# One block on one core: weight buffers of 8 KB a partition, and the experts' weights in loads of 1 MB

## The chip, the cores and the metric

The kernel runs on 1 core of one Trainium2 chip. The metric is the device time of one execution in microseconds (us). The median of 3 runs is 1118.22 us (1117.07 to 1118.95).

## The reference

One decoder block on x of 512 tokens x 1024 channels, in float32. Three stages matter here.

- Projections: `u = RMSNorm(h)`, one wide product `u @ W_in`, a Mamba-2 SSD branch and a causal depthwise convolution branch on its columns, each with an output product, then the mixed result through `W_o`, added to h.
- Experts: `h + HierMoE(RMSNorm(h))`. A router picks one of 4 groups and two of its 8 experts for each token. An expert is `(silu(x @ w_gate) * (x @ w_up)) @ w_down` with inner width 512, so its three matrices are 2 MB each; 32 experts make 201.3 MB.
- Last stage: `h + (p @ W_ple_proj) * sigmoid(RMSNorm(h) @ W_ple_gate)`, then a final RMSNorm.

## The kernel before

The whole kernel is written out as a list of **units** (`unit`, L247). A unit has one or more weight loads and a function that issues its matmuls. `step` (L342) runs the units in order: it first splits the weights of later units, then lets `pump` (L261) issue loads, then the matmuls of its own unit, then `after` (L328) the jobs tied to that unit and as many of the floating `tasks` as a running credit allows. The order that comes out is the order on each engine; nothing reorders it later.

**Buffers.** All weights, and several other tiles, live in one pool of 22 **pages** of 4 KB a partition (`page`, L224; `PAGES`, L70). `state["room"]` counts the pages that `pump` may still fill with loads; `free(n)` gives n back or, with a negative n, takes them away. In the projections the room is 4 and later 8; before the experts it grows to 20.

**Two kinds of units.** In the projections and in the last stage a load of 512 KB (`raw`) is split in two parts: ACT casts it to the high part `wh` (`split_hi`, L275, the cast in L289), DVE subtracts to get the low part `wl` (`split_lo`, L293), each a page; PE then multiplies three times. The number of units that the split runs ahead is 2 in the projections and `BT["hi"]` = 6 from the experts on (L349). The experts' units are `plain`: PE reads the loaded float32 directly (L353 to L356) and the pages are freed after the unit's matmuls.

**Experts.** 32 experts stand in 7 groups of one or two quads; a quad is 4 strips of 32 slots, shared by 2 or 3 experts. For a quad there are 8 gate/up units (`gu_unit`, L1186: two matrices, four quarters of the contraction) and 4 down units (`d_unit`, L1199), each with one load of 512 KB per expert. With `(p k) n -> p k n` a load takes 4 KB that lie together for each partition. Between them stand, as jobs, `hid_act`, `hid_mul`, `hid_tr` (SiLU on ACT, product on DVE, transposition on PE) and `y_hi`, `y_lo` (scaled output on ACT and DVE); as tasks `disp` (tokens of the next group to slots), `back` and `combine` (the result back to tokens). `hot` writes the one-hot matrices of the next group, one page a group. The routing, `order0` to `order8`, are jobs of the first units (L1666). The first group's experts are fixed, the others are read from a register on SP.

**Before the last group** (one quad of three experts) come the two units of the ple projection (`p_unit`, L1308: 24 products each), and jobs that take room away: `free` of -1, -2, -8 and -4 pages (L1325 to L1341), since p, its parts and four output pages need pages.

**Last stage.** Eight units `e_unit` (L1431), 512 KB each: four for the first 512 columns, whose products run unit by unit, four for the second, whose products all run in the last unit (`prod`, token block by token block, k in order). The main body splits three of them between the transposes `e_tr` (L1812 to L1815). Behind the first half stand `e_gate` (tanh on ACT, two DVE instructions), `e_gain` on POOL and `e_sq` (a square on ACT).

All loads of weights go through SP's queue (L269), p and small tensors through POOL's. Matmuls, DVE copies and sums that go through a helper show as L120 in the profile.

Of the kernel before, what the change touches and what calls it, by code (L numbers as in the profile page):

```python
# [17 lines left out]
D = 1024  # L18
T = 512
# [47 lines left out]
    RANK[_b] = _i  # L67

_CST = {}
PAGES = 22  # L70
BT = dict(room=8, raw=20, hi=6, page=1.27, mm=1.75, cap=5.0, sp=5, fill=[1.8, 0.9], late=[14, 3])


TUNE = dict(
# [62 lines left out]
def tile_hybrid(ctx: ExitStack, tc: tile.TileContext, x, p, chan, rowv, rows, cst, w_in, w_ssd, w_conf, w_o,  # L137
# [83 lines left out]
            nc.scalar.copy(dsth, src)  # L221
            nc.vector.tensor_sub(dstl, src, dsth)

    def page(shape, dt):  # L224

        return st(shape, dt, "w", PAGES)

    def pages(n, dt):
        return Parts([page([128, 2, T], dt) for _ in range(n)], 2)

    al = slice(None)
    LAG = TUNE["lag"]
# [7 lines left out]
    jobs = defaultdict(list)  # L240
    state = {"pairs": 0, "n": 0, "load": 0, "room": 4, "split": 0, "lo": 0, "credit": 0, "top": 0}

    def load(src):
        loads.append(dict(src=src))
        return loads[-1]

    def unit(src, mms, cost=0.0, plain=False):  # L247
        srcs = [] if src is None else src if isinstance(src, list) else [src]
        units.append(dict(lds=[load(s) for s in srcs], mms=mms, cost=cost, plain=plain))
        return len(units) - 1  # L250

    def job(n, f, *a):
# [8 lines left out]
    def pump():  # L261
        while state["load"] < len(loads):
            ld = loads[state["load"]]
            if state["room"] <= 0:
                return
            src = ld["src"]()
            state["room"] -= 1
            ld["t"] = page([128] + list(src.shape[1:]), F32)
            nc.sync.dma_start(ld["t"], src)  # L269
            state["load"] += 1  # L270

# [3 lines left out]
    def split_hi():  # L275
        n = state["split"]
        if n >= len(units):
            return False
        u = units[n]
        if u["lds"] and not u["plain"]:  # L280
            ld = u["lds"][0]
            if "t" not in ld:
                pump()
            if "t" not in ld:
                assert n >= NB
                return False
            u["raw"] = ld["t"]
            u["wh"], u["wl"] = [page(list(u["raw"].shape), F32R) for _ in range(2)]
            nc.scalar.copy(u["wh"], u["raw"])  # L289
        state["split"] += 1  # L290
        return True
# [36 lines left out]
    def after(u):  # L328
        n = state["n"]
        issue(n - 0.5)  # L330
        issue(n)
        state["n"] = n + 1
        state["credit"] = min(state["credit"] + BT["page"] * len(u["lds"]) - u["cost"], BT["cap"])
        while True:
            t = min((t for t in tasks if t[0] <= n), key=lambda t: t[1], default=None)
            if t is None or (state["credit"] <= 0 and t[1] > n):
                break
            tasks.remove(t)
            state["credit"] -= t[2]
            t[3](*t[4])  # L340

    def step():  # L342
        n = state["n"]
        top = state["top"]
        if n < NB:
            while state["split"] <= min(max(n + 2, 2 * n - NB + BT["sp"]), top):
                split()
        else:
            while state["split"] <= min(top, n + BT["hi"]) and split_hi():  # L349
                split_lo()  # L350
        pump()
        u = units[n]
        if u["plain"]:  # L353
            ws = [ld["t"] for ld in u["lds"]]
            u["mms"](ws)
            free(len(ws))  # L356
        elif u["mms"] is not None:
            u["mms"](u["wh"], u["wl"])
        after(u)
# [44 lines left out]
        return first  # L404


    xl, xn = [Parts([page([128, D], F32) for _ in range(NT)], 1) for _ in range(2)]
    ss = st([128, NT], F32, "ss", 2)
    for c in range(NT):
        nc.sync.dma_start(xl[al, c, al], x[c * 128:(c + 1) * 128, :])  # L410
# [528 lines left out]
    def ln3(j):  # L939
        if j == 0:  # L940
            cm["h"] = pages(4, F32R)
            cm["l"] = []
        t = st([128, T], F32, "k2", 4)
        nc.vector.tensor_mul(t, cj[j], ln["rs"])
        nc.scalar.activation(t, t, AF.Silu, bias=ch("lnb", j), scale=ch("lng", j))
        nc.scalar.copy(cm["h"][al, j, al], t)
        if j < 6:
            cm["l"].append(st([128, T], F32R, "cj", 9))
        elif j == 6:
            lo = page([128, 2, T], F32R)  # L950
            cm["l"].extend(lo[:, i, :] for i in range(2))
        nc.vector.tensor_sub(cm["l"][j], t, cm["h"][al, j, al])

# [61 lines left out]
    pj = {}  # L1015

    def p_load():
        pj["p"] = page([128, NT, PLE], F32)
        nc.gpsimd.dma_start(pj["p"], p.rearrange("(c t) n -> t c n", t=128))

    def p_tr(k):
        pt = acc()
        for c in range(NT):
            nc.tensor.transpose(pt[:, c * 128:(c + 1) * 128], pj["p"][:, c, k * 128:(k + 1) * 128], ident)
        if k == 0:
            pj["h"], pj["l"] = [page([128, 2, T], F32R) for _ in range(2)]
        split_t(pj["h"][:, k, :], pj["l"][:, k, :], pt, None)

    def p_mm(c, wh, wl):
# [6 lines left out]

    def p_out(n, c):
        if c % 2 == 0:
            pj["o", n, c // 2] = page([128, 2, T], F32)
        nc.scalar.activation(pj["o", n, c // 2][:, c % 2, :], pj.pop("s"), AF.Copy, scale=0.5)  # L1040

    NO = len(units)
# [143 lines left out]
    def gu_unit(gi, q, i, kp):  # L1186
        quad = GROUPS[gi][q]

        def mms(ws):
            if kp == 0:  # L1190
                PG[gi, q, i] = acc()
            x = XT[gi, kp]
            for kk in range(2):
                strips(PG[gi, q, i], x[:, kk, q * QS:(q + 1) * QS], [w[:, kk, :] for w in ws], quad,
                       kp == 0 and kk == 0, kp == 3 and kk == 1)
        return unit([lambda b=m[0]: weights((eg, eu)[i], b)[:, 2 * kp:2 * kp + 2, :] for m in quad], mms, BT["mm"],
                    True)

    def d_unit(gi, q, f):  # L1199
        quad = GROUPS[gi][q]  # L1200

        def mms(ws):
            if f == 0:
                PY[gi, q] = [acc2(), acc2()]
            for n in range(2):
                strips(PY[gi, q][n], HT[gi, q][:, f, :], [w[:, 0, n * 512:(n + 1) * 512] for w in ws], quad, f == 0,
                       f == 3)
        return unit([lambda b=m[0]: weights(ed, b)[:, f:f + 1, :] for m in quad], mms, BT["mm"], True)

    def hid_act(gi, q):  # L1210
        t = st([128, DE], F32, "k2", 4)
# [9 lines left out]
    def hid_tr(gi, q):  # L1221
# [4 lines left out]
        nc.scalar.copy(t, pt.rearrange("p (f s) -> p f s", s=QS))  # L1226
        HT[gi, q] = t

    def hot(gi, q):
        if q == 0:  # L1230
            G["oh", gi] = page([128, NT, 2 * QS], F32R)
        for b, j0, ns in GROUPS[gi][q]:
            r = ns * ST
            o = q * QS + j0 * ST
            nc.vector.tensor_tensor(G["oh", gi][:, :, o:o + r], cs_("slot")[:, None, :r].to_broadcast([128, NT, r]),
                                    R["pos"][:, :, b:b + 1].to_broadcast([128, NT, r]), op=OP.is_equal)

    def hot_first(c):

        if c == 0:  # L1240
            G["oh", 0] = page([128, NT, 2 * QS], F32R)
        w = [128, 4, 2 * ST]
        nc.vector.tensor_tensor(G["oh", 0][:, c].rearrange("p (j s) -> p j s", s=2 * ST),
                                cs_("slot")[:, None, :2 * ST].to_broadcast(w),
# [70 lines left out]
    def fill_now(room):  # L1315
        fill_pe(state["n"], room)

    combined = NB + 9
    for gi, g in enumerate(GROUPS):
        last = gi == len(GROUPS) - 1  # L1320
        first = len(units)
        if last:
            for n in range(2):
                p_unit(n)
            job(first - 10, free, -1)  # L1325
            job(first - 9, p_load)
            job(first - 8, free, -2)
            for k in range(2):
                job(first - 4 + k, p_tr, k)
            job(first - 3, free, -8)  # L1330
        for q in range(len(g)):
            for kp in range(4):
                for i in range(2):
                    u = gu_unit(gi, q, i, kp)
            job(u - 1, hid_act, gi, q)
# [2 lines left out]
            job(u, hid_tr, gi, q)  # L1338
            job(u, fill_now, BT["fill"][1])
            if last:  # L1340
                job(u - 3, free, -4)  # L1341
            for f in range(4):
                u = d_unit(gi, q, f)
            task(combined, u - 1, 1.4, back, gi, q)
            for n in range(2):
                job(u, y_hi, gi, q, n)
                job(u, y_lo, gi, q, n)
# [4 lines left out]
            continue  # L1352
        for n in range(2):
            for c in range(NT):
                task(u + 1, u + 9, 0.23 * 2 * len(g), combine, gi, c, n)
        combined = u + 10
        o = first + (BT["late"][0] if gi == 0 else BT["late"][1])
        for q in range(len(GROUPS[gi + 1])):
            job(o + q, hot, gi + 1, q)
        for kp in range(4):  # L1360
            task(o + 2, u, 0.115 * 16, disp, gi + 1, kp)
    for i in range(3):
        unit(None, None)
    NC = len(units)
# [45 lines left out]

    def e_gain(c):

        E["o", c] = page([128, D], F32)
        ns = slice(0, 512)
        nc.gpsimd.tensor_mul(E["o", c][:, ns], hh_["h"][:, c, ns], E["gf"][:, ns])

# [247 lines left out]

    state["top"] = NE
    for i, f in enumerate((order0, order4, order1, order2, order3, order5, order6, order7, order8)):  # L1666
        job(NB + 2 + i, f)
    pts = [acc() for _ in range(4)]
    for a in range(2):
        for k in range(4):  # L1670
            disp_mm(0, k, pts[k], a)
    for k in range(4):
        disp_out(0, k, pts[k])
        step()
        step()
    run(NC)

    W32 = [128, NEXP]
# [207 lines left out]
```

## Time and profile before

| | us |
|---|---|
| median of 3 runs | 1118.22 |
| lowest, highest | 1117.07, 1118.95 |
| the profiled execution, its own time | 1116.51 |
| its span (first to last instruction) | 1114.8 |
| PE, DVE, ACT busy in the span | 1029.8, 561.6, 345.1 |
| HBM read | 252.83 MB |

The mean granted TensorE clock is 0.982 of full speed. An engine's busy time is a mean over stages with different limits, so it is read stage by stage: projections to about 526 us, routing to 542 us, experts to about 1055 us, last stage to the end. Ends of matmuls are modelled, so a busy PE is not a PE at its peak.

### The profile page before, as it was taken

The page shows a single profiled execution, that of the slowest core. Times are in us where ns is not written, and L with a number is a line of the kernel's source. Part 1 is how long each engine was busy: PE and PEld are TensorE (multiplying, and loading weights), DVE is VectorE, ACT ScalarE, POOL GpSimd, SP SyncE. Part 2 cuts the span into 40 slices and gives each one's busy share as a digit, 9 for nine tenths or more (in the row PEclk, how much of TensorE's full clock was granted, in tenths as well). Part 3 has the DMA queues.
Part 4 walks back from the last instruction along what each step waited for, and adds up shares of the span by engine and source line. Part 5 has one row for each costly group of instructions (what it writes and reads, how often), then busy time and mean ns, then how long its engine had stood idle before and what let it go on. Part 6 is the DMA issues. An engine that isn't in the chain of part 4 may idle for free. (4 is left out here: it accounts for less than half of the span.)

```text
span 1114.8 us, 16449 instructions
## 1 busy us (share of the span) xinstructions
PE 1029.8 (92%) x6262; PEld 665.0 (60%) x6262; DVE 561.6 (50%) x1004; ACT 345.1 (31%) x646; POOL 14.7 (1%) x32
## 2 busy tenths in 40 slices
PE   5999999999989999997999999989989899659796
PEld 4788899877868887886553434425335235125375
DVE  6689998897889955655322203112021121021475
ACT  5443356767442245334111100101101101021263
POOL 1000000000000000000000000000000000000011
PEclk9999999999999999999899999999999999969998
DMA  9323232202223341373599899999999999968801
GB/s 268 101 82 87 79 94 59 76 19 76 76 57 107 95 148 66 127 302 113 192 409 359 304 411 408 409 409 409 408 409 408 409 409 409 404 241 328 319 24 75
DMA packets 123314, 256.04 MB, mean 230 GB/s; under 512 B 7856, under 2 KB 65216, under 8 KB 123232
## 3 DMA queue, kind: packets, MB, share of 16 engines
q1 hardware_dynamic: 122544, 252.74, 61.6%
q0 software_dynamic: 688, 2.22, 0.7%
q8 instruction: 50, 0.82, 0.3%
q14 instruction: 32, 0.26, 0.1%
HBM read 252.83 MB, written 2.10 MB: 229 GB/s over the span
## 5 line engine op out<-in xcount | busy, mean ns | idle before, releaser
L120 PE MATMUL acc<-uh,w 128*128 128x512 f32 x704 | 230.5, 400 | 0.8 <-DVE ul L120 0.8
L120 PE MATMUL acc<-w,cj 128*32 128x512 f32 x1664 | 214.7, 596 | 8.1 <-DMA w<-eu 4.3
L120 PE MATMUL acc<-w,uh 128*128 128x256 f32 (+2 forms) x752 | 162.1, 325 | 1.1 <-DVE w L120 0.9
L120 PEld LDWEIGHTS acc<-uh,w 128*128 128x128 f32 x704 | 132.3, 188 | 31.2 <-issue 1.7
L120 PE MATMUL acc<-w,m 128*32 128x512 f32 (+1 forms) x960 | 133.2, 569 | 10.2 <-ACT m L1226 5.3
L120 DVE TENSOR_TENSOR w<-w 128x1024 fp32r<-128x1024 f32 x86 | 104.4, 1220 | 75.6 <-ACT w L289 62.9
L120 PE MATMUL acc<-ul,w 128*128 128x512 f32 x352 | 137.4, 390 | 0.0
L120 PEld LDWEIGHTS acc<-w,cj 128*32 128x32 f32 x1664 | 52.2, 109 | 140.2 <-issue 94.1
L120 PEld LDWEIGHTS acc<-w,uh 128*128 128x128 f32 x752 | 118.2, 193 | 26.3 <-issue 15.3
L120 DVE SCALAR_TENSOR_TENSOR cj<-glu,chan,cj 128x512 f32<-128x512 f32 x180 | 130.8, 747 | 2.2
L120 PE MATMUL acc<-w,ul 128*128 128x256 f32 (+2 forms) x488 | 117.3, 307 | 0.6 <-DVE ul L120 0.6
L289 ACT CAST w<-w 128x1024 fp32r<-128x1024 f32 x86 | 89.6, 1054 | 75.1 <-PE acc L120 44.1
L120 PE MATMUL acc<-w 128*128 128x512 f32 x384 | 98.9, 394 | 3.1 <-ACT w L289 2.4
L120 PEld LDWEIGHTS acc<-w,m 128*32 128x32 f32 (+1 forms) x960 | 43.4, 122 | 82.8 <-issue 44.3
L120 DVE TENSOR_TENSOR k<-k,acc 128x512 f32<-128x512 f32 x21 | 19.1, 910 | 138.9 <-PE acc L120 138.8
L120 PEld LDWEIGHTS acc<-w 128*128 128x128 f32 x384 | 71.5, 188 | 21.4 <-ACT w L289 2.8
L120 DVE TENSOR_TENSOR Z<-Z,acc 128x512 f32<-128x512 f32 x64 | 43.3, 686 | 79.9 <-PE acc L120 79.9
L120 PEld LDWEIGHTS acc<-w,ul 128*128 128x128 f32 x488 | 77.0, 188 | 6.8 <-DVE ul L120 1.4
L120 PEld LDWEIGHTS acc<-ul,w 128*128 128x128 f32 x352 | 66.2, 188 | 14.9 <-issue 1.7
L1258 ACT COPY cj<-acc 128x512 f32<-128x512 f32 (+1 forms) x28 | 15.6, 556 | 163.4 <-PE acc L120 163.4
L120 PE MATMUL acc<-ident,k 128*128 128x128 f32 x116 | 17.9, 282 | 28.6 <-DVE k L120 26.8
L120 DVE SCALAR_TENSOR_TENSOR w<-glu,chan,w 128x512 f32<-128x512 f32 x60 | 42.9, 747 | 0.7
(267 smaller groups left out, 864.6 us busy)
## 6 DMA issues: line engine op xcount, KB each, us to landing
w<-eg SPq DMA_DIRECT2D x128, 512.0 KB, 10.1
w<-eu SPq DMA_DIRECT2D x128, 512.0 KB, 10.1
w<-ed SPq DMA_DIRECT2D x128, 512.0 KB, 10.1
w<-w_in SPq DMA_DIRECT2D x52, 512.0 KB, 3.7
w<-w_ssd_out SPq DMA_DIRECT2D x8, 512.0 KB, 3.9
w<-w_conf_out SPq DMA_DIRECT2D x8, 512.0 KB, 3.6
w<-w_o SPq DMA_DIRECT2D x8, 512.0 KB, 3.5
w<-w_ple_gate SPq DMA_DIRECT2D x8, 512.0 KB, 10.3
```

The costliest lines, as they stand in the source:

```text
L120: return f(*a, **k)
L289: nc.scalar.copy(u["wh"], u["raw"])
L1258: nc.scalar.copy(t, pt[:, :2 * w].rearrange("p (k s) -> p k s", k=2))
```

## The change

The pool becomes 11 buffers of 8 KB a partition. `page` hands out halves: the first request with a key takes a buffer, the second with the same key takes its other half. `wh` and `wl` of one unit share a buffer, so do two consecutive raw loads, pairs of `x`, of the outputs `po` and `eo`, and so on. The experts' loads are `wide`: 1 MB each, a whole buffer, 8 KB together for each partition, two pages of room. There are half as many experts' units, each twice as large (4 gate/up and 2 down units a quad). The one-hot matrices of all groups live in the two halves of one buffer. The numbers that count in units are set anew: `hi` 6 to 1, `late`, the due units of the tasks, the jobs of the routing, and the frees before the last group.

```diff
-PAGES = 22
-BT = dict(room=8, raw=20, hi=6, page=1.27, mm=1.75, cap=5.0, sp=5, fill=[1.8, 0.9], late=[14, 3])
+PAGES = 11
+BT = dict(room=8, raw=20, hi=1, page=1.27, mm=3.5, cap=5.0, sp=5, fill=[1.8, 0.9], late=[7, 2])
...
-    def page(shape, dt):
-
-        return st(shape, dt, "w", PAGES)
+    pend = {}
+
+    def page(shape, dt, key):
+        v = pend.pop(key, None)
+        if v is None:
+            v = st([128, 4 * T], dt, "w", PAGES)
+            pend[key] = v[:, 2 * T:]
+            v = v[:, :2 * T]
+        return v.rearrange("p (a b) -> p a b", b=shape[2]) if len(shape) == 3 else v
...
-            if state["room"] <= 0:
+            if state["room"] <= (1 if ld["wide"] else 0):
                 return
             src = ld["src"]()
-            state["room"] -= 1
-            ld["t"] = page([128] + list(src.shape[1:]), F32)
+            if ld["wide"]:
+                state["room"] -= 2
+                ld["t"] = st([128] + list(src.shape[1:]), F32, "w", PAGES)
+            else:
+                state["room"] -= 1
+                ld["t"] = page([128] + list(src.shape[1:]), F32, "raw")
             nc.sync.dma_start(ld["t"], src)
...
-            u["wh"], u["wl"] = [page(list(u["raw"].shape), F32R) for _ in range(2)]
+            u["wh"], u["wl"] = [page(list(u["raw"].shape), F32R, n) for _ in range(2)]
...
-            free(len(ws))
+            free(2 * len(ws))
...
-        return unit([lambda b=m[0]: weights((eg, eu)[i], b)[:, 2 * kp:2 * kp + 2, :] for m in quad], mms, BT["mm"],
+            for kk in range(4):
+                k = 4 * kp + kk
+                strips(PG[gi, q, i], XT[gi, k // 2][:, k % 2, q * QS:(q + 1) * QS], [w[:, kk, :] for w in ws], quad,
+                       k == 0, k == KD - 1)
+        return unit([lambda b=m[0]: weights((eg, eu)[i], b)[:, 4 * kp:4 * kp + 4, :] for m in quad], mms, BT["mm"],
...
-        return unit([lambda b=m[0]: weights(ed, b)[:, f:f + 1, :] for m in quad], mms, BT["mm"], True)
+        return unit([lambda b=m[0]: weights(ed, b)[:, 2 * fp:2 * fp + 2, :] for m in quad], mms, BT["mm"], True)
...
+    def one_hot(gi):
+        if gi == 0:
+            G["ohs"] = st([128, 2, NT, 2 * QS], F32R, "w", PAGES)
+        return G["ohs"][:, gi % 2]
...
-            job(first - 10, free, -1)
-            job(first - 9, p_load)
-            job(first - 8, free, -2)
+            job(first - 6, free, -2)
+            job(first - 5, p_load)
+            job(first - 5, free, -2)
             for k in range(2):
-                job(first - 4 + k, p_tr, k)
-            job(first - 3, free, -8)
+                job(first - 3 + k, p_tr, k)
+            job(first - 2, free, 2)
+            job(first - 2, free, -8)
...
             if last:
-                job(u - 3, free, -4)
-            for f in range(4):
+                job(u - 1, free, -2)
+            for f in range(2):
                 u = d_unit(gi, q, f)
             task(combined, u - 1, 1.4, back, gi, q)
+            if last:
+                job(u - 1, free, -2)
...
-            job(o + q, hot, gi + 1, q)
+            job(o, hot, gi + 1, q)
...
-        job(NB + 2 + i, f)
+        job(NB + (i + 1) // 2, f)
```

## Rows read from the trace of the kernel before

**Rows 1.** The page, part 2: DMA busy tenths and GB/s in 40 slices.
```profile
DMA  9323232202223341373599899999999999968801
GB/s 268 101 82 87 79 94 59 76 19 76 76 57 107 95 148 66 127 302 113 192 409 359 304 411 408 409 409 409 408 409 408 409 409 409 404 241 328 319 24 75
```

**Rows 2.** Stretches: length, busy us (count) of PE, PEld, DVE, ACT, POOL; PEclk, DMA share, GB/s.
```profile
20.00:526.00 506.00, 496.78 (x2528) 409.12 (x2526) 405.58 (x645) 234.30 (x457) 2.97 (x9) 1.00 0.33 102
...
542.00:597.00 55.00, 51.60 (x444) 23.13 (x440) 10.59 (x40) 7.76 (x14) 0.00 (x0) 0.97 0.98 382
597.00:645.00 48.00, 48.00 (x385) 22.95 (x378) 12.25 (x26) 6.77 (x11) 0.00 (x0) 1.00 0.91 330
645.00:965.00 320.00, 300.15 (x2147) 122.22 (x2146) 52.35 (x106) 34.59 (x58) 0.76 (x1) 1.00 1.03 408
965.00:987.00 22.00, 2.52 (x12) 0.38 (x10) 3.38 (x3) 2.09 (x2) 0.00 (x0) 0.66 0.86 330
987.00:1020.00 33.00, 32.02 (x200) 16.49 (x200) 5.04 (x8) 7.92 (x13) 0.00 (x0) 0.91 0.72 249
1020.00:1045.00 25.00, 23.54 (x166) 9.60 (x162) 5.11 (x10) 1.77 (x3) 0.00 (x0) 1.00 1.03 409
```

**Rows 3.** Waits, 645 to 966 us: engine, line, waited for, us in total, times, longest.
```profile
PEld acc L120 <- DMA w<-ed: 23.4, 28, 1.1
```

**Rows 4.** The chain that ended last, one piece: start, us, what.
```profile
1059.58 34.47 PE acc L120 x155
```

**Rows 5.** Waits, 966 to 990 us.
```profile
DVE w L120 <- ACT w L289: 34.7, 1, 34.7
...
PE acc L120 <- DVE k L120: 19.5, 1, 19.5
ACT w L289 <- DMA w<-w_ple_proj: 18.5, 1, 18.5
```

**Rows 6.** DMA packets: 13:29 (512 B), 1044:1050 (2 KB), 700:900 us (4 KB).
```profile
DMA packets 9210, 4.64 MB, mean 290 GB/s; under 512 B 144, under 2 KB 9210, under 8 KB 9210
...
DMA packets 1203, 2.32 MB, mean 387 GB/s; under 512 B 72, under 2 KB 72, under 8 KB 1203
...
DMA packets 22408, 81.75 MB, mean 409 GB/s; under 512 B 2489, under 2 KB 2489, under 8 KB 22392
```

**Rows 7.** The page, part 6, DMA issues: KB each, us from issue to landing.
```profile
w<-eg SPq DMA_DIRECT2D x128, 512.0 KB, 10.1
...
w<-w_o SPq DMA_DIRECT2D x8, 512.0 KB, 3.5
...
w<-p POOLq DMA_DIRECT2D x1, 512.0 KB, 8.1
```

**Rows 8.** Timeline, PE, 762 us: start, us, instruction.
```profile
762.06 5.36 PE L120 MATMUL acc<-w,cj 128*32 128x512 f32 x48
```

**Rows 9.** Timeline, ACT and DVE, last stage: start, us, instruction, idle before.
```profile
1058.09 1.04 ACT L289 CAST w<-w 128x1024 fp32r<-128x1024 f32 x1
...
1081.53 0.69 ACT L1406 ACTIVATE k<-acc,et 128x512 f32<-128x512 f32 x1 [0.17 <-PE acc L120]
1082.93 0.69 ACT L1406 ACTIVATE k<-acc,et 128x512 f32<-128x512 f32 x1 [0.71 <-PE acc L120]
...
1089.23 0.63 ACT L1372 ACTIVATE k<-Z 128x512 bf16<-128x512 f32 x1 [1.54 <-DVE Z L120]
...
1057.64 1.23 DVE L120 TENSOR_TENSOR w<-w 128x1024 fp32r<-128x1024 f32 x1
...
1081.54 0.69 DVE L120 TENSOR_TENSOR Z<-Z,k 128x512 f32<-128x512 f32 x1
...
1087.51 1.69 DVE L120 TENSOR_TENSOR Z<-Z,k 128x512 f32<-128x512 f32 x1
```

**Rows 10.** One more stretch, columns as in rows 2.
```profile
530.00:540.00 10.00, 10.00 (x64) 9.75 (x64) 7.52 (x21) 1.76 (x3) 0.00 (x0) 0.74 0.01 2
```

**Rows 11.** Waits of PE, 20 to 526 us.
```profile
PE acc L120 <- ACT w L289: 2.4, 1, 2.4
```

More of the change, by code (lines that the diff above doesn't have):

```diff
@@ L222, in split_t @@
             nc.vector.tensor_sub(dstl, src, dsth)
-    def page(shape, dt):
-        return st(shape, dt, "w", PAGES)
+    pend = {}
[6 more added lines that the diff above has]
+        return v.rearrange("p (a b) -> p a b", b=shape[2]) if len(shape) == 3 else v
     def pages(n, dt):
-        return Parts([page([128, 2, T], dt) for _ in range(n)], 2)
+        k = object()
+        return Parts([page([128, 2, T], dt, k) for _ in range(n)], 2)
     al = slice(None)
@@ L241, in tile_hybrid, with load @@
     state = {"pairs": 0, "n": 0, "load": 0, "room": 4, "split": 0, "lo": 0, "credit": 0, "top": 0}
-    def load(src):
-        loads.append(dict(src=src))
+    def load(src, wide):
+        loads.append(dict(src=src, wide=wide))
         return loads[-1]
@@ L248, in unit @@
         srcs = [] if src is None else src if isinstance(src, list) else [src]
-        units.append(dict(lds=[load(s) for s in srcs], mms=mms, cost=cost, plain=plain))
+        units.append(dict(lds=[load(s, plain) for s in srcs], mms=mms, cost=cost, plain=plain))
         return len(units) - 1
@@ L332, in after @@
         state["n"] = n + 1
-        state["credit"] = min(state["credit"] + BT["page"] * len(u["lds"]) - u["cost"], BT["cap"])
+        state["credit"] = min(state["credit"] + BT["page"] * (2 if u["plain"] else 1) * len(u["lds"]) - u["cost"], BT["cap"])
         while True:
@@ L404, in tokproj @@
         return first
-    xl, xn = [Parts([page([128, D], F32) for _ in range(NT)], 1) for _ in range(2)]
+    xl, xn = [Parts([page([128, D], F32, "x") for _ in range(NT)], 1) for _ in range(2)]
     ss = st([128, NT], F32, "ss", 2)
@@ L949, in ln3 @@
         elif j == 6:
-            lo = page([128, 2, T], F32R)
+            lo = page([128, 2, T], F32R, "lo")
             cm["l"].extend(lo[:, i, :] for i in range(2))
@@ L1017, in p_load @@
     def p_load():
-        pj["p"] = page([128, NT, PLE], F32)
+        pj["p"] = page([128, NT, PLE], F32, "p")
         nc.gpsimd.dma_start(pj["p"], p.rearrange("(c t) n -> t c n", t=128))
@@ L1025, in p_tr @@
         if k == 0:
-            pj["h"], pj["l"] = [page([128, 2, T], F32R) for _ in range(2)]
+            pj["h"], pj["l"] = [page([128, 2, T], F32R, "ph") for _ in range(2)]
         split_t(pj["h"][:, k, :], pj["l"][:, k, :], pt, None)
@@ L1038, in p_out @@
         if c % 2 == 0:
-            pj["o", n, c // 2] = page([128, 2, T], F32)
+            pj["o", n, c // 2] = page([128, 2, T], F32, "po")
         nc.scalar.activation(pj["o", n, c // 2][:, c % 2, :], pj.pop("s"), AF.Copy, scale=0.5)
@@ L1191, in mms, with d_unit @@
                 PG[gi, q, i] = acc()
[L1192 to L1195, printed above, removed]
-        return unit([lambda b=m[0]: weights((eg, eu)[i], b)[:, 2 * kp:2 * kp + 2, :] for m in quad], mms, BT["mm"],
+            for kk in range(4):
[3 more added lines that the diff above has]
+        return unit([lambda b=m[0]: weights((eg, eu)[i], b)[:, 4 * kp:4 * kp + 4, :] for m in quad], mms, BT["mm"],
                     True)
-    def d_unit(gi, q, f):
+    def d_unit(gi, q, fp):
         quad = GROUPS[gi][q]
         def mms(ws):
-            if f == 0:
+            if fp == 0:
                 PY[gi, q] = [acc2(), acc2()]
-            for n in range(2):
-                strips(PY[gi, q][n], HT[gi, q][:, f, :], [w[:, 0, n * 512:(n + 1) * 512] for w in ws], quad, f == 0,
-                       f == 3)
-        return unit([lambda b=m[0]: weights(ed, b)[:, f:f + 1, :] for m in quad], mms, BT["mm"], True)
+            for f in (2 * fp, 2 * fp + 1):
+                for n in range(2):
+                    strips(PY[gi, q][n], HT[gi, q][:, f, :], [w[:, f % 2, n * 512:(n + 1) * 512] for w in ws], quad,
+                           f == 0, f == 3)
+        return unit([lambda b=m[0]: weights(ed, b)[:, 2 * fp:2 * fp + 2, :] for m in quad], mms, BT["mm"], True)
     def hid_act(gi, q):
@@ L1227, in hid_tr @@
         HT[gi, q] = t
+    def one_hot(gi):
+        if gi == 0:
+            G["ohs"] = st([128, 2, NT, 2 * QS], F32R, "w", PAGES)
+        return G["ohs"][:, gi % 2]
     def hot(gi, q):
         if q == 0:
-            G["oh", gi] = page([128, NT, 2 * QS], F32R)
+            G["oh", gi] = one_hot(gi)
         for b, j0, ns in GROUPS[gi][q]:
@@ L1240, in hot_first @@
         if c == 0:
-            G["oh", 0] = page([128, NT, 2 * QS], F32R)
+            G["oh", 0] = one_hot(0)
         w = [128, 4, 2 * ST]
@@ L1316, in fill_now @@
         fill_pe(state["n"], room)
-    combined = NB + 9
+    combined = NB + 4
     for gi, g in enumerate(GROUPS):
@@ L1324, in tile_hybrid @@
                 p_unit(n)
-            job(first - 10, free, -1)
-            job(first - 9, p_load)
-            job(first - 8, free, -2)
+            job(first - 6, free, -2)
+            job(first - 5, p_load)
+            job(first - 5, free, -2)
             for k in range(2):
-                job(first - 4 + k, p_tr, k)
-            job(first - 3, free, -8)
+                job(first - 3 + k, p_tr, k)
+            job(first - 2, free, 2)
+            job(first - 2, free, -8)
         for q in range(len(g)):
-            for kp in range(4):
+            for kp in range(2):
                 for i in range(2):
@@ L1354, in tile_hybrid @@
             for c in range(NT):
-                task(u + 1, u + 9, 0.23 * 2 * len(g), combine, gi, c, n)
-        combined = u + 10
+                task(u + 1, u + 5, 0.23 * 2 * len(g), combine, gi, c, n)
+        combined = u + 5
         o = first + (BT["late"][0] if gi == 0 else BT["late"][1])
         for q in range(len(GROUPS[gi + 1])):
-            job(o + q, hot, gi + 1, q)
+            job(o, hot, gi + 1, q)
         for kp in range(4):
-            task(o + 2, u, 0.115 * 16, disp, gi + 1, kp)
+            task(o + 1, u, 0.115 * 16, disp, gi + 1, kp)
     for i in range(3):
@@ L1411, in e_gain @@
     def e_gain(c):
-        E["o", c] = page([128, D], F32)
+        E["o", c] = page([128, D], F32, "eo")
         ns = slice(0, 512)
@@ L1673, in tile_hybrid @@
         disp_out(0, k, pts[k])
-        step()
-        step()
+        if k % 2:
+            step()
+            step()
     run(NC)
```

## The prediction

> **What bounds the kernel now.** I read the slices of the page first: three stages show. Up to some 525 us the DMA is mostly idle, from there to 1045 us most slices move 400 GB/s and more, and in the last 60 us the DMA rests again [rows 1]. The table by stretches says which engine sets the pace in each [rows 2]. From 20 to 526 us PE is busy 496.78 of 506 us: the projections are bound by TensorE, and the loads hide behind it. From 542 to 645 us the stream of the experts' weights runs at 382 and 330 GB/s while PE hardly pauses: PE holds the 20 pages, and the loads wait for room. From 645 to 965 us the stream runs at 408 GB/s without a gap, and TensorE waits for loads, 23.4 us for ed's alone [rows 3]: here the DMA is the bound. From 965 to 1020 us it falls to 330 and 249 GB/s, then it is back at 409 to 1045 us. The last 60 us are a chain through PE, ACT and DVE, with 34.47 us of uninterrupted matmuls in it [rows 4].
>
> The hole at 965 us is an order on two engines: six units ahead of the ple projection the split of its weights is queued. ACT waits 18.5 us for that load, DVE 34.7 us behind ACT, and the multiply of the hidden layer stands behind DVE's subtract, so PE waits 19.5 us [rows 5]. When it resumes, buffers come free too slowly to fill the queue.
>
> **The change part by part.** The sum is made against the profiled execution (1116.51 us, span 1114.8), which lies 1.7 us under the median of 1118.22; a difference is carried over to the median.
>
> *Rows of 8 KB.* 384 loads of 512 KB become 192 of 1 MB, with 8 KB instead of 4 KB together in each partition. No row shows 8 KB, so I extend the three sizes that ran back to back on all 16 engines: 512 B at 290 GB/s, 2 KB at 387, 4 KB at 409 [rows 6]. Time of one row on one engine, 16 x size / rate: 28.2, 84.7 and 160.2 ns. From 512 B to 2 KB each KB adds 37.6 ns, from 2 to 4 KB 37.8 ns: a straight line with some 9 ns fixed. Four more KB give 160.2 + 151.0 = 311.2 ns, so 421 GB/s. What can gain is the stream behind the stretch that PE holds: 202.4 MB (experts and the projection's 1.05) less the 20 pages of 0.524 MB held at 542 us, 55 us x 382 and 48 us x 330, which leaves 155.1 MB. At 409 GB/s that is 379.2 us, at 421 it is 368.4: **-10.8 us**. Bounds: 0 (a row moves as two of 4 KB) and -13.4 (424 GB/s, if more than the row's fixed part goes with the smaller number of loads). I take 421, since both steps of size lie on one line.
>
> The Trainium skill (DMA: Bandwidth & Descriptors, Bandwidth, "Why small descriptors are slow") puts the fixed cost at about 3 cycles a packet beside one cycle for 32 bytes; a 4 KB row then loses 2.3%, and 8 KB would win 1.2%, as an estimate 4.3 us in place of 10.8, and the time would be 1117.1. The trace disagrees so far: 3 cycles beside 128 are 3.5 ns of a row's 151, and its fixed part is 9.
>
> *Issue.* SP starts half as many loads. Their issue hides behind a queue that is 10.1 us from issue to landing against 3.5 us for an unqueued load [rows 7]; without that cover it would be a fraction of a microsecond a load. A wide load waits until two pages of room are there, and what stands behind it on SP waits with it; that is counted in the tail below. I take 0.
>
> *Split one unit ahead (hi 6 to 1), the frees before the last group.* ACT's cast for the projection now comes just before the last down unit, after the hidden layer's work of that quad, so the 19.5 us wait of PE goes. Behind the waiting cast stand now y_hi on ACT and y_lo on DVE, for which only the later combines wait. What is late next is room. A wide unit costs PE 3.6 us (48 matmuls take 5.36 us, 16 of them one old unit, [rows 8]). By hand, at 421 GB/s, time 0 being the landing of the first down unit's third load in the last but one group: the loads pumped so far keep the stream going to 12.5 us; PE ends the two down units at 3.2 and 10.7 us; room is now 10 pages, five buffers, while a unit of this quad takes three. The projection's two units are 24 products each, 5.6 us (six take 1.40 us, [rows 9]), and hold PE to 22 us, when the five buffers are full. The first gate unit ends at 25.7 us, and a load starts 2.1 us after its issue (3.5 less 1.36 us of transfer): a gap of 5.4 us. Each later release leaves a smaller one: 1.3 before the last up load, 2.8 and 2.8 us at the down loads, as room shrinks to four and three buffers. Together 12.3 us of idle DMA. Before it was 22 us x (1 - 330/409) + 33 us x (1 - 249/409) = 17.2 us [rows 2]. The last unit is 3.6 us instead of 1.8, which adds 1.6 us behind its last landing. **-3.3 us**, between -10 (gaps hidden by the tasks between the units) and +3.
>
> *Split one unit ahead, last stage.* The same number rules the splits here. Before, all eight weights of the gate product were split in its first steps; now only the first four are (main asks for them between the e_tr), and those of the second half come one a step. The third and fourth of the second half then stand on DVE behind the two instructions of each of the four e_gate, on ACT behind their four tanh and, the fourth, behind the four squares of e_sq; PE's first product waits for them, and everything to the end waits for PE. PE ends the first half at 1082.9 us (the last tanh starts on it). It needs the third low part 13 products later, at 1085.9 us. DVE ends the e_gate at 1087.51 + 1.69 = 1089.20 us and its subtract takes 1.23: 1090.4 us, a wait of 4.5 us. Beside POOL's multiply the adds took 1.69 us instead of 0.69, so the subtract may take 1 us more. The fourth: ACT's last square starts at 1089.23 us, then a cast of 1.04 and the subtract, some 0.5 us behind PE again [rows 9]. I take **+5.5 us** (4.5 to 6.5). Behind such a pause the granted clock may be at the lower level: in the 10 us after the routing's pause it averaged 0.74, 2.6 us lost at most [rows 10]; I take **+1.0 us**.
>
> *8 KB buffers in the projections.* Halves of one buffer come free together: a raw half up to one unit (5.6 us) later, with four loads ahead and 3.5 us to landing. The high and low weights of one unit end with the same matmuls. I take 0; PE's pauses cover it, and without them each late cast would be PE's wait. The nearest row is one wait of 2.4 us for a cast in 506 us [rows 11], so 0 to +4.
>
> *The rest.* The routing jobs, one-hots and dispatches keep their place within about 1 MB of weights, in a stretch that PE holds (542 to 645 us): 0, between -3 and +3. The load of p on POOL has two wide units, some 15 us, to land; it took 8.1 [rows 7]. The one-hots' shared buffer and both halves at one job: 0, DVE is mostly idle there.
>
> Sum: -10.8 - 3.3 + 5.5 + 1.0 = -7.6; 1116.5 becomes 1108.9, and on the median 1110.6 us.
>
> **The rivals.** *8 KB rows are no faster.* The fixed part of a row may belong to something that does not halve. For it: nothing here has moved 8 KB rows in a stream, and 2 to 4 KB gave only 6%; against it: the line. Then -3.3 + 6.5 = +3.2: **1121.4**, slower. It decides below 412.6 GB/s, where the rate wins under 3.2 us. The skill's 3 cycles would leave it just above that point.
>
> *The late splits are hidden.* If PE is paced by something else in the second half 6.5 us fall away: **1104.1**. For it: DVE has little queued behind the e_gate; against it: PE's 34.47 us without a break.
>
> *The shared buffers hold the projections back.* 76 casts; each late by 0.10 us eats the gain, at 0.2 us the time is **1126**. Against it: PE's pauses total 9 of 506 us.
>
> *The clock falls in the stream.* With three loads a unit PE's bursts come 2.5 us apart instead of 1.3. At the lower level (1.2 of 2.4 GHz) a group's 24 quarter units (43 us) and the rest would take some 120 us where the stream needs 75, over four groups some +180: **1285**. Against it: the clock stayed at 1.00 through 320 us of short bursts [rows 2]. The Trainium skill (TensorE: Matmul & The Clock Gate, Part 1) has the clock halve when the array idles; here it was 0.66 around a 20 us pause and 1.00 between bursts.
>
> **How the numbers follow.** Forecast 0.52, no faster rows 0.20, hidden splits 0.18, held projections 0.07, clock 0.03. The likeliest case alone runs from 1102 to 1117 (bounds of its tail and waits). The range must reach both neighbours: 1099 to 1122. A measurement of this kernel tells about 0.2% (2.2 us) from nothing. Faster 0.66: 0.46 of the forecast, the hidden splits, 0.02 of the others. Same 0.09: 0.05 of the forecast, the rest from rows only a little faster. Slower 0.25: the other two rivals and most of the case without faster rows.
>
> **What would show it.** Between 650 and 950 us the GB/s read 421; the same 409 kills the first term. Packets in a stretch of the stream halve, and none lies under 8 KB but the small ones. ACT's wait for the ple projection is a few us, PE's wait on the multiply of the hidden layer is about 1 us. Holes of 1 to 6 us in the DMA up to the last down load. In the last stage a wait of PE for DVE's w of some 5 us, 25 us before the end; its absence puts the second rival right. From 20 to 526 us PE busy within 3 us of before. I am wrong if the stream is at 421 and the time is not under 1116, or if it is at 409 and the time is.

## The result and the profile after

The changed kernel takes 1109.47 us (median of 4 runs, 1109.12 to 1111.59) beside 1117.64 us of the kernel before in the same session: a ratio of **0.9926** (95% interval 0.9911 to 0.9941), 8.2 us less. The prediction was 1110.6 us. The profiled execution took 1109.12 us with a span of 1107.4. The total came out as forecast; its parts did not.

The page of the changed kernel, part 2: DMA busy tenths and GB/s in 40 slices.

```profile
DMA  9323232202224323265199999999999999999401
GB/s 268 99 69 107 77 87 67 77 1 77 68 65 118 86 77 114 77 234 222 39 382 388 392 376 423 420 421 421 421 421 420 421 421 420 418 377 422 178 1 76
```

Beside [rows 1] the plateau is higher, 420 to 423 in place of 408 to 411, and the dent at its end is nearly gone (418, 377, 422 where before had 404, 241, 328, 319). The stretches of [rows 2], in the changed kernel (columns as there):

```profile
20.00:526.00 506.00, 495.41 (x2487) 407.03 (x2486) 400.00 (x619) 229.70 (x447) 2.97 (x9) 0.99 0.33 99
542.00:597.00 55.00, 53.04 (x448) 27.77 (x450) 14.53 (x55) 10.19 (x16) 0.00 (x0) 0.95 0.76 308
597.00:645.00 48.00, 47.22 (x384) 22.24 (x380) 11.22 (x21) 5.78 (x10) 0.00 (x0) 1.00 0.95 376
645.00:965.00 320.00, 288.66 (x2222) 129.00 (x2215) 54.16 (x112) 36.17 (x62) 0.76 (x1) 0.98 1.01 419
965.00:987.00 22.00, 18.97 (x112) 8.57 (x105) 6.28 (x7) 6.88 (x11) 0.00 (x0) 1.00 1.02 416
987.00:1020.00 33.00, 31.13 (x210) 16.77 (x212) 7.15 (x13) 4.62 (x8) 0.00 (x0) 0.98 0.95 389
```

The first row is a trap, and the prediction fell into it: PE is as busy as before, yet it has done less, 2487 matmuls in place of 2528 (and DVE 619 instructions in place of 645). A window of fixed times can't show that work has moved out of it. So I cut every profile at two instructions instead: ACT's one instruction on `prev` in the routing, and the 16 transposes that open the last stage. The changed kernel's timeline has them at

```profile
537.41 0.20 ACT L1558 ACTIVATE prev<-prev 128x16 f32<-128x16 f32 x1
...
1038.65 3.00 PE L120 MATMUL acc<-ident,Z 128*128 128x128 f32 x16 [3.53 <-DVEq L1704]
```

and the timeline of the kernel before at

```profile
527.80 0.20 ACT L1536 ACTIVATE prev<-prev 128x16 f32<-128x16 f32 x1
...
1055.29 1.97 PE L120 MATMUL acc<-ident,Z 128*128 128x128 f32 x16 [2.22 <-DVEq L1681]
```

Cut so, for every kernel of this study (us, one profiled execution each; ratio of the timed runs to before's beside them, with its 95% interval):

| kernel | up to routing | routing to last stage | last stage | span | ratio |
|---|---|---|---|---|---|
| before | 527.8 | 527.5 | 59.5 | 1114.8 | 1 |
| changed | 537.4 | 501.2 | 68.8 | 1107.4 | 0.9926 (0.9911 to 0.9941) |
| last_splits | 538.1 | 505.4 | 59.8 | 1103.2 | 0.9867 (0.9850 to 0.9883) |
| room3 | 530.7 | 502.6 | 68.6 | 1101.8 | 0.9862 (0.9838 to 0.9885) |
| rows4 | 538.5 | 514.4 | 68.8 | 1121.7 | 1.0037 (1.0017 to 1.0057) |
| two_loads | 536.3 | 511.8 | 68.6 | 1116.6 | 1.0001 (0.9991 to 1.0010) |
| both_fix | 529.0 | 505.2 | 59.7 | 1093.8 | 0.9777 (0.9753 to 0.9801) |
| split_early | 537.5 | 504.6 | 68.6 | 1110.7 | 0.9938 (0.9915 to 0.9962) |
| before_hi1 | 530.8 | 511.0 | 60.0 | 1101.7 | 0.9862 (0.9837 to 0.9887) |
| before_room3 | 530.3 | 527.1 | 59.6 | 1117.0 | 0.9995 (0.9983 to 1.0008) |

The change wins 26.3 us in the experts' stage, where 14.1 were forecast, and loses 9.6 in the projections (0 forecast) and 9.2 in the last stage (6.5). Below, a difference of two ratios is turned into us by the 1118 us of before; with these intervals it is good to 2 to 4 us. A stage's length comes from one execution: last_splits has the changed kernel's program up to the last stage, and its experts' stage was 4.1 us longer, so lengths in this table are good to some 4 us.

### The profile page after: what moved, and what is told of

Its sections match the earlier page's. It is cut to its first block, busy times and chain, and to the rows that moved or that the text cites. A ratio compares the mean times of both kernels' runs of the same rounds, so it can differ in the third digit from the quotient of the medians.

```text
span 1107.4 us, 15682 instructions
## 1 busy us (share of the span) xinstructions
PE 1017.9 (92%) x6262; PEld 675.5 (61%) x6262; DVE 562.2 (51%) x1004; ACT 344.6 (31%) x646; POOL 15.5 (1%) x32
## 5 line engine op out<-in xcount | busy, mean ns | idle before, releaser
L120 PE MATMUL acc<-w,cj 128*32 128x512 f32 x1664 | 203.4, 608 | 17.6 <-DMA w<-eu 10.7
L120 PEld LDWEIGHTS acc<-w,cj 128*32 128x32 f32 x1664 | 56.2, 112 | 143.3 <-issue 105.3
L120 PE MATMUL acc<-w,m 128*32 128x512 f32 (+1 forms) x960 | 126.8, 574 | 13.7 <-DMA w<-ed 8.8
L120 PE MATMUL acc<-w 128*128 128x512 f32 x384 | 102.0, 405 | 3.0 <-ACT w L302 2.4
L120 PEld LDWEIGHTS acc<-w 128*128 128x128 f32 x384 | 74.0, 194 | 22.0 <-ACT w L302 2.8
L1226 ACT ACTIVATE k<-acc 128x512 f32<-128x512 f32 x13 | 7.8, 598 | 165.2 <-PE acc L120 165.2
L1277 ACT COPY cj<-acc 128x512 f32<-128x512 f32 (+1 forms) x28 | 15.6, 555 | 81.9 <-PE acc L120 81.9
```

The lines of the kernel that those rows point to most:

```text
L120: return f(*a, **k)
L1226: nc.scalar.activation(t, PG.pop((gi, q, 0)), AF.Silu)
L1277: nc.scalar.copy(t, pt[:, :2 * w].rearrange("p (k s) -> p k s", k=2))
```

## The experiments

### The row or the load: rows4 and two_loads

Loads of 1 MB whose partition rows are two runs of 4 KB:

```diff
-        return unit([lambda b=m[0]: weights((eg, eu)[i], b)[:, 4 * kp:4 * kp + 4, :] for m in quad], mms, BT["mm"],
+        def src(b):
+            w = weights((eg, eu)[i], b)
+            return w.rearrange("p (a c b) n -> p c a (b n)", a=2, c=2)[:, kp] if gi else w[:, 4 * kp:4 * kp + 4, :]
+        return unit([lambda b=m[0]: src(b) for m in quad], mms, BT["mm"],
...
-        return unit([lambda b=m[0]: weights(ed, b)[:, 2 * fp:2 * fp + 2, :] for m in quad], mms, BT["mm"], True)
+        return unit([lambda b=m[0]: weights(ed, b)[:, fp::2, :] for m in quad], mms, BT["mm"], True)
```

The order of the products follows the rows (those lines are left out here).

> The changed kernel, its loads still 1 MB each and as many, but of two runs of 4 KB a partition instead of one of 8 KB (the first group's gate and up weights stay as they are). Theory of the row: the rate follows the row, so the stream between 700 and 950 us falls from 421 to 409 GB/s and the time rises by 8 to 11 us, to 1117.5 to 1120.5. Rival (the load): the rate follows the size of the load, so it stays near 421 and the time within 2 us of 1109.5.

And the same buffers filled by two loads each:

```diff
-            nc.sync.dma_start(ld["t"], src)
+            if ld["wide"]:
+                m = src.shape[1] // 2
+                for i in range(2):
+                    nc.sync.dma_start(ld["t"][:, i * m:(i + 1) * m], src[:, i * m:(i + 1) * m])
+            else:
+                nc.sync.dma_start(ld["t"], src)
```

> The changed kernel, each buffer of 1 MB filled by two loads of 512 KB with rows of 4 KB, issued one behind the other. Both theories of the rate give 409 GB/s between 700 and 950 us and 1117.5 to 1120.5 us; against the kernel with two runs of 4 KB in one load it tells what the number of loads costs by itself: 0 if the issue is hidden, up to 3 us where the queue starts from empty behind the routing and in the last group.

The DMA between 700 and 940 us, in the changed kernel (packets; then issues: KB each, us to landing):

```profile
DMA packets 13849, 100.96 MB, mean 421 GB/s; under 512 B 1539, under 2 KB 1539, under 8 KB 1539
...
w<-eg SPq DMA_DIRECT2D x32, 1024.0 KB, 15.2
```

in rows4

```profile
DMA packets 25395, 98.08 MB, mean 409 GB/s; under 512 B 1493, under 2 KB 1493, under 8 KB 25378
...
w<-eg SPq DMA_DIRECT2D x31, 1024.0 KB, 15.8
```

and in two_loads

```profile
DMA packets 26892, 98.10 MB, mean 409 GB/s; under 512 B 2987, under 2 KB 2987, under 8 KB 26874
...
w<-eg SPq DMA_DIRECT2D x63, 512.0 KB, 10.2
```

The rate follows the row, and the load's size does nothing to it: 409 GB/s with loads of 1 MB and of 512 KB alike, 421 with 8 KB together. rows4 is 12.4 us slower than the changed kernel, two_loads 8.4 us; 8 to 11 were expected of both. That the two differ by 4 us I had not expected; it is the other way round from a cost of issue, and stays open.

### The last stage: last_splits

```diff
-            while state["split"] <= min(top, n + BT["hi"]) and split_hi():
+            while state["split"] <= min(top, n + (6 if n >= NE else BT["hi"])) and split_hi():
```

> The changed kernel with one edit: in the last stage alone the split runs 6 units ahead again, as before. Theory: the four splits that stand behind the squares and the gate's DVE pairs cost PE one wait of 6.5 us for DVE's w at 1070 us, and the clock after it 1 to 2 us more; so the wait goes and the time falls by 6.5 to 8.5 us, to 1101 to 1103 us. Rival: the first half's squares and the adds on DVE (1.68 us beside POOL) pace the stage whatever the order; then PE waits for something else instead and the time falls by less than 3 us.

What it was to remove, in the changed kernel. Waits of PE, 1036 to 1108 us:

```profile
PE acc L120 <- DVE w L120: 6.5, 1, 6.5
```

The timeline of its DVE behind the first half's products:

```profile
1061.92 1.23 DVE L120 TENSOR_TENSOR w<-w 128x1024 fp32r<-128x1024 f32 x1 [5.00 <-ACT w L302]
...
1073.52 1.67 DVE L120 TENSOR_TENSOR Z<-Z,k 128x512 f32<-128x512 f32 x1
1075.11 1.21 DVE L120 TENSOR_TENSOR w<-w 128x1024 fp32r<-128x1024 f32 x1
```

and of its PE:

```profile
1069.33 0.50 PE L120 MATMUL acc<-w,uh 128*128 128x512 f32 x1
1076.37 0.80 PE L120 MATMUL acc<-w,uh 128*128 128x512 f32 x1 [6.55 <-DVE w L120]
```

The third subtract of the second half starts as the last add of the gate ends, and PE starts as the subtract ends: the step the prediction named. ACT's timeline of last_splits has the four casts ahead of the squares:

```profile
1049.48 2.95 ACT L302 CAST w<-w 128x1024 fp32r<-128x1024 f32 x3
...
1054.28 1.05 ACT L302 CAST w<-w 128x1024 fp32r<-128x1024 f32 x1
```

Of the waits of PE, 1043 to 1104 us, only the one for the stage's first input is left:

```profile
PE acc L120 <- DVEq L1704: 3.5, 1, 3.5
```

The stage is back at 59.8 us, 9.0 less; the ratio gives 6.6 us, at the lower end of the 6.5 to 8.5 expected. The span falls by only 4.2 us, since the experts' stage of this execution was 4.1 us longer.

### The projections: room3 and before_room3

Where the 9.6 us are lost is read from the casts `w <- w` on ACT. In the changed kernel's timeline they come in pairs, one late, one at once:

```profile
339.47 1.05 ACT L302 CAST w<-w 128x1024 fp32r<-128x1024 f32 x1 [6.30 <-PE acc L120]
...
342.39 1.05 ACT L302 CAST w<-w 128x1024 fp32r<-128x1024 f32 x1 [1.37 <-DVE w L120]
...
409.77 1.04 ACT L302 CAST w<-w 128x1024 fp32r<-128x1024 f32 x1 [5.34 <-PE acc L120]
412.77 0.63 ACT L928 ACTIVATE k<-cj 128x512 f32<-128x512 f32 x1 [1.95 <-DVE cj L120]
```

and PE's, behind the last of these:

```profile
413.45 1.05 PE L120 MATMUL acc<-ones,k 128*128 128x1 f32 x8 [2.93 <-ACT k L928]
```

The cast itself is rarely what PE wants. What PE wants stands behind it, on two engines: DVE waits 7.16 us for the cast at 409.77 before it can subtract, the input of the square of L928 stands on DVE behind that subtract, so the square starts 1.95 us after the cast has ended, and PE waits 2.9 us for the square. Behind the wait PE's matmuls are slower for a while, 12 of them in 4.59 us (granted clock 0.68 from 413.4 to 418.8 us) where 7 of the same shape, six microseconds later, take 1.85:

```profile
414.37 4.59 PE L120 MATMUL acc<-w 128*128 128x512 f32 x12
...
420.50 1.85 PE L120 MATMUL acc<-w 128*128 128x512 f32 x7
```

Matched with the kernel before matmul by matmul, the lag of PE is 1.0 us up to 309 us, 3.4 from 310, 4.9 from 340 and 9.6 from 418: it comes in steps, not with each cast. The first and the third step (1.0 and 1.5 us) are no doing of the change, as the last section shows. The second (2.4 us, with a wait of PE of 1.6 us for DVE's `w`) and the fourth (4.7 us, the wait of 2.9 and the slow matmuls behind it) stand in all five kernels that have the changed projections as they are (2.3 to 2.4 and 4.7 to 5.5 us) and in no other: some 7 us. Waits of PE, 270 to 435 us, in the changed kernel:

```profile
PE acc L120 <- ACT k L928: 2.9, 1, 2.9
...
PE acc L120 <- DVE w L120: 2.1, 2, 1.6
```

My theory counts buffers. From unit 33 on `ssd_norm` holds eight pages, `late` and `gate_sig1` two each; loads may have 4, and three units' high and low weights 6: 22 pages exactly, 11 buffers exactly. But a raw pair keeps its buffer until its second half is split, so four pages of loads can sit in three buffers. Then one unit's weights are a buffer short, and its cast waits for PE. One page less for loads should cure it:

```diff
-            job(n, free, 2)
+            job(n, free, 3)
...
     job(0, halve)
+    job(30, free, -1)
```

> The changed kernel with one edit: from unit 30 of the projections to the end of the SSD output product, loads may hold 3 pages instead of 4. Theory: pairs of raw loads that share a buffer hold up to three buffers where room counts two, so every second cast on ACT waits some 7 us for PE to end a unit, and what stands behind the cast makes PE wait; with one page less the casts' waits for PE fall from 54.6 us to under 20, the projections end 4 to 7 us earlier, and the time is 1103 to 1106 us. Rival: loads come too late with three pages; then the casts wait for the DMA instead and the time is 1109 to 1113. Second rival: the 9.6 us are mostly the clock's; then no change within 1.5 us.

Waits of ACT, 270 to 425 us, in the changed kernel:

```profile
ACT w L302 <- PE acc L120: 52.0, 9, 7.5
```

and in room3:

```profile
ACT w L302 <- DVE w L120: 35.0, 5, 7.8
...
ACT w L302 <- PE acc L120: 10.9, 7, 3.1
```

The casts' waits for PE are nearly gone (those for DVE come early enough and delay nobody). PE's waits of 2.9 and 1.6 us are gone, the routing comes at 530.7 us in place of 537.4, and the time falls by 7.2 us. Whether this is a matter of pairs or of a pool that is short in both kernels, the same edit in the kernel before tells:

> The kernel before with the edit of the projections alone: 3 pages instead of 4 for loads from unit 30 to the end of the SSD output product. Theory of the pairs: what cost the changed kernel 7 us is that two raw loads, and the high and low weights, must each come free before their buffer does; with single pages 4 loads, 12 long-lived pages and 6 of high and low weights are 22 exactly, so one page less for loads gains nothing: 0.999 to 1.001. Rival: the pool is simply short of room in both kernels, and the casts' waits for PE (44.1 us here, 54.6 in the changed kernel) cost both; then they fall under 25 us and the time falls by 3 to 6 us: 0.995 to 0.997.

It gives 0.9995 (0.9983 to 1.0008): nothing. In that stretch the casts of the kernel before wait 44.1 us for PE,

```profile
ACT w L289 <- PE acc L120: 44.1, 11, 4.5
```

and with one page less still 37.7:

```profile
ACT w L289 <- PE acc L120: 37.7, 9, 4.5
```

So a cast's wait for PE is not harmful by itself: with single pages the casts wait up to 4.5 us, and nothing is lost; with shared buffers up to 7.5 us, and 7 us are lost. That sharing makes the pool too short for four pages of loads is shown by the two runs together. That it is the raw pairs which hold the missing buffer, and not other shared halves, is argued from the count; no run parts them.

### The split's place: before_hi1 and split_early

The kernel before, with `hi` 1 in the experts' stage alone:

```diff
-            while state["split"] <= min(top, n + BT["hi"]) and split_hi():
+            while state["split"] <= min(top, n + (6 if n >= NE else 1)) and split_hi():
```

> The kernel before with one edit: the split runs 1 unit ahead in the experts' stage and 6 in the last stage, all else (4 KB rows, loads of 512 KB, the frees where they were) as before. Theory of the trace: PE's wait of 19.5 us at 965 us falls under 6 us and the stream's end is 9 to 13 us earlier: 0.988 to 0.992 of before. Theory of the prediction: the room is too small behind it in any case, 3 us: 0.997. Rival: one narrow unit ahead is too late for the projection's weights, and PE waits 3 us twice for the split: 0.993 to 1.000.

Stretches and waits (960 to 1000 us) of before_hi1:

```profile
965.00:987.00 22.00, 16.95 (x92) 4.94 (x93) 4.44 (x6) 5.13 (x8) 0.00 (x0) 1.00 1.03 406
987.00:1020.00 33.00, 33.00 (x210) 18.14 (x209) 7.39 (x11) 5.42 (x10) 0.00 (x0) 1.00 0.96 372
```

```profile
DVE w L120 <- ACT w L289: 6.2, 1, 6.2
ACT w L289 <- DMA w<-w_ple_proj: 5.9, 1, 5.9
...
PE acc L120 <- DVE k L120: 1.2, 1, 1.2
```

PE's wait for the hidden layer's product is 1.2 us in place of the 19.5 of [rows 5], the DMA keeps 406 and 372 GB/s where [rows 2] has 330 and 249, and the kernel is 15.4 us faster than before. The theory of the prediction and the rival both fall. **One number in the kernel before, without wide loads or shared buffers, brings more than the whole change.** It is more than the theory of the trace allowed (9 to 13 us) and over four times the prediction's term.

The mirror of it in the changed kernel, 3 wide units ahead up to the last stage:

> The changed kernel with one edit: up to the last stage the split runs 3 wide units ahead instead of 1 (as many bytes of weights as the 6 narrow units of before), in the last stage 1 as in the changed kernel. Theory of the trace: the split's place is worth some 12 us at the end of the stream, so PE waits 15 to 20 us again for the hidden layer's product, the DMA falls to 200 to 300 GB/s behind it, and the time is 8 to 14 us over the changed kernel's: 1.000 to 1.005 of before. Theory of the prediction: 3.3 us, 0.995 to 0.997. Rival: the frees, not the split's place, kept the stream going; then under 2 us, 0.992 to 0.994.

It gives 0.9938, 1.3 us over the changed kernel and within its interval. Both theories miss; the result lies where the rival had it, that in the changed kernel the frees keep the stream going. It does not contradict before_hi1, for the edit hardly moved the split. ACT's timeline has the projection's first cast there at

```profile
979.88 1.05 ACT L302 CAST w<-w 128x1024 fp32r<-128x1024 f32 x1 [10.61 <-issue]
```

and in the changed kernel at

```profile
978.91 1.04 ACT L302 CAST w<-w 128x1024 fp32r<-128x1024 f32 x1 [4.01 <-DMA w<-w_ple_proj]
```

The split can't be written before its load, and the frees of the changed kernel let that load out only when the hidden layer's work is already queued. So the cast moved by one place, not ahead of the hidden layer. Its place in the changed kernel is fixed by the frees as much as by `hi`; no run parts the two there.

### Both repairs together: both_fix

The changed kernel with the diffs of last_splits and room3.

> The changed kernel with both edits: the split 6 units ahead again in the last stage, and 3 pages instead of 4 for loads from unit 30 of the projections to the end of the SSD output product. Theory: the two losses lie in different stages and on the path, so the gains add: 0.9867 and 0.9862 of before against 0.9926 for the changed kernel make 0.9803, some 1097 us where before is 1119. Rival: the last group's end hangs on where the clock stands and takes part of it back; then 0.983 to 0.986.

0.9777 (0.9753 to 0.9801), a median of 1095.49 us where before has 1119.85 in the same session: 2.2% faster than before, 1.5% faster than the change. The repairs lie in different stages and add: 0.9803 was expected, and the difference to it is within the noise of the four ratios. In its last stage PE waits once, 3.5 us for the first input, and the routing comes at 529.0 us.

## Why the prediction was right in sum and wrong in parts

**Rows of 8 KB: right.** 421 GB/s forecast, 421 measured; by the rate, 16 x 8192 B / 421 GB/s is the 311 ns of a row that the straight line gave. -10.8 us were forecast; the experiments give 8.4 and 12.4 us, and both_fix against before_hi1, the two repaired kernels with and without 8 KB, 9.5. The first rival (no faster rows) falls, and with rows4 its other form too, that fewer loads would make the gain: there they are as few, and the rate is 409. The Trainium skill (DMA: Bandwidth & Descriptors, Bandwidth, "Why small descriptors are slow") has 3 cycles a packet, which would have made 1.2% of rate; the step from 4 to 8 KB measured 2.9%. The Trainium skill (DMA: Bandwidth & Descriptors, Bandwidth, "Measured") advises batching DMAs to 1 MiB or more, from figures of loads that GpSimd issued; in SP's queue here, kept full, loads of 512 KB and 1 MB with the same rows both ran at 409.

**Issue at nothing: right as far as shown**; twice the loads in two_loads was no slower than rows4.

**The split one unit ahead, and the room behind it: mechanism right, size wrong by 12 us.** -3.3 us were forecast, with -10 as the bound; before_hi1 gained 15.4. The wait of 19.5 us went as said; the waits of the changed kernel, 960 to 1000 us (ACT's is the cast's):

```profile
ACT w L302 <- DMA w<-w_ple_proj: 4.0, 1, 4.0
...
PE acc L120 <- DVE k L120: 1.2, 1, 1.2
```

The step that failed is the hand run behind it, "What is late next is room", with four gaps of 12.3 us in all. The changed kernel had, in the two stretches of that hole, 22 us x (1 - 416/421) + 33 us x (1 - 389/421) = 2.8 us of idle DMA. SP's timeline shows how:

```profile
967.75 7.47 SPq L282 DMA_DIRECT2D w<-eg  x3
980.43 6.77 SPq L282 DMA_DIRECT2D w<-eu  x3
993.24 3.90 SPq L282 DMA_DIRECT2D w<-eg  x3
997.38 3.19 SPq L282 DMA_DIRECT2D w<-eu  x3
1000.81 11.50 SPq L282 DMA_DIRECT2D w<-ed  x6
```

The hand run let the next load wait for the end of the first gate unit. It left at 993.24, when the projection's second unit ended and that gate unit began, and from there none waited long: the projection itself gives buffers back, which the hand run had left out. I had counted only what the gate units free. (That these were its buffers is argued from the order of the program; no run took them away.) The second failure is one of bounds: I set -10 for "gaps hidden", though the sum's own terms without any gap, -17.2 + 1.6, make -15.6, close to the 15.4 of before_hi1.

**The last stage: mechanism right, some 2 us short.** The two forecast waits are one of 6.55 us (5.5 forecast, 4.5 to 6.5), on the instruction named. Behind it the granted clock was 0.50, the lower of its two levels (1.2 GHz), from 1076.4 to 1080 us, and 0.96 from 1080 to 1085: some 2 us lost, where I took 1.0. By its length the stage cost 9.0 us, 6.6 and 9.5 by the ratios (last_splits against the change, both_fix against room3), beside 6.5 forecast. The rival of hidden splits falls.

**8 KB buffers in the projections: wrong.** I took 0, with +4 as the bound; by the ratios they cost 7.2 us (room3 against the change) and 10.1 (both_fix against last_splits). The step said that halves come free together up to one unit later, and that "four loads ahead" cover it. The loads did; by the count, the buffer that they held too long was missing for the weights. And I priced a late cast by PE's wait for the cast, where the price lies with what stands behind it on ACT and DVE. The third rival had the mechanism, at 0.07, and spread it over 76 casts; it came in two places (at 310 us, and from 413 to 418). The Trainium skill (Perfetto Trace Analysis, Identifying Performance Opportunities, Optimization Strategy) has the same gap repeating, on the engine that should be saturated, as a possible sign of too little SBUF for the next tile. Here the repeating gap was on ACT, some 7 us at every second cast, while PE, the engine to keep busy, had two single waits more than before; and less room for loads was the cure.

**The rest: 0 forecast.** Between 552 and 655 us, the same work 9.6 us later, the stream ran at 382 and 378 GB/s in place of 382 and 330, some 2.3 MB more. But two_loads, with 4 KB rows and all else changed, needs 511.8 us from the routing to the last stage, and before_hi1, with nothing but the split's place changed, 511.0: by that nothing is left over, as far as such lengths can tell.

**The clock in the stream**: 0.98 from 645 to 965 us; the fourth rival falls. (Its 1285 does not come out of its own terms: 1110.6 + 180 is 1290.6.)

So the sum of the parts as the experiments give them, -10 for the rows, -15.4 for the split's place, some +8 each for projections and last stage, is -9.4; measured -8.2. The forecast of -7.6 was near because the tail's missed 12 us paid for the 8 us that the projections lost and the last stage's underrated 2. The forecast's case did happen, and its time was partly luck.

## What to carry to other kernels

Cut two profiles at the same instructions, not at the same times: a stretch that stays full hides that its work has shifted. When two tiles share a buffer, count buffers by the later of the two releases, and look at what is queued, on every engine, behind the instruction that will wait for one. And when one change turns several numbers, try each alone on the old kernel first: here the lead of a split was worth 15 us by itself, and the change with its two losses repaired 24 to 25.

## What the runs showed of the hardware

The clock can differ between executions of one program in one place. Behind PE's pause of 2.4 us near 330 us come 24 matmuls. In the profiled execution of the kernel before, the granted clock from 330 to 340 us was 1.00, and the timeline has

```profile
327.96 0.77 PE L120 MATMUL acc<-w 128*128 128x512 f32 x2 [2.42 <-ACT w L289]
329.22 5.31 PE L120 MATMUL acc<-w 128*128 128x512 f32 x22 [0.49 <-DVE w L120]
```

In before_hi1, whose program is the same up to the experts, it was 0.75, and the 24 took

```profile
328.44 9.02 PE L120 MATMUL acc<-w 128*128 128x512 f32 x24 [2.41 <-ACT w L289]
```

So of the 9.6 us by which the routing is later in the pair of profiles, some 1.6 (6.89 us for the 22 in the changed kernel) are no doing of the change, nor is the 1.0 us by which its PE lags from 20 us on: that lag lies between -0.1 and 1.6 us in all kernels here, old projections and changed ones alike. The routing of the three kernels with the old projections lies at 527.8, 530.3 and 530.8, that of the five with the changed ones at 536.3 to 538.5. A single profile of each side would not have told that.
